# ScalarE and VectorE in written order for the first norm, squares on both engines, weight parts, and the small loads on GpSimd's queue

## The chip, the cores and the metric

The kernel runs on one core of one Trainium2 chip. The metric is the device time of one execution in microseconds (us), the median of several runs. A lower time is better.

## What is computed

One layer of a hybrid block over x of 512 x 1024 in float32. Cut to what matters:

```
xn = RMSNorm(x) * g_mix
u  = xn @ W_in                       # [q | k | v | rnn_x | rnn_gate | gate_A | gate_B], 1024 columns each
A  = chunked band attention(q, k, v) with a relative bias
xc = causal depthwise conv (width 4) of rnn_x, with bias
B  = RG-LRU(xc; block-diagonal gates W_r, W_i, softplus(-lambda)) * GeLU(rnn_gate)
mix = (sigmoid(gate_A) * (A @ W_a) + sigmoid(gate_B) * (B @ W_b)) @ W_o
h  = x + mix;  h = h + SwiGLU(RMSNorm(h));  out = RMSNorm(h)
```

## The kernel before

Every product is made of three matmuls on float32r parts: each operand is split into an upper part `hi` (rounded) and a lower part `lo = x - hi`, and `mm3` (L72 to L76) adds hi\*hi (L74), hi\*lo (L75) and lo\*hi (L76). `split` (L78 to L81) makes `hi` on ScalarE (L80) and `lo` on VectorE (L81). Weights come in chunks of 256 columns (`xr0`, `gr0`, `ga0`, `gb0`, `xr2` and so on), each in two loads of 4 x 128 rows; the tile of a split half chunk is `whl`, of which there are four buffers, that of its load is `raw`, of which there are three. So the halves of chunk `ga0` take the buffers that `xr0` had, and those of `gb0` the buffers of `gr0`, once TensorE has done with them.

The beginning goes like this. x comes in four tiles of 128 rows (`xt`). `squares` (L369) sums the squares of a tile on ScalarE; `norm_half` (L339) takes two tiles: square root on ScalarE (L334), reciprocal on VectorE (L336), scaling on VectorE (L345), transposes on TensorE (L353) into PSUM (`pt_mix`), then the upper part of `xnT` with the norm's weights on ScalarE (L357) and the lower part on VectorE (L358). As soon as the first 256 rows are there, `first_half` projects them with chunks `xr0` and `gr0` into four PSUM tiles (`po_xr` and `po_gr`, two columns of 128 each); the other 256 rows follow into the same tiles. Behind it the small vectors (`vr`: convolution, biases, lambda) are transposed (`vp`, L405) into `vc`, softplus of lambda is worked out in small steps (`sp_...`, L432 to L457), and the gates' block weights are split into `wrg_r` and `wrg_i` (upper part on ScalarE, L466, lower part on GpSimd, L467).

Then comes the loop over channels. `rnn_conv` (L477) makes the convolution `xc`: one tap on ScalarE (L483), three on VectorE (L485), each of which reads `po_xr` in PSUM. `rnn_gelu` (L491) works on `po_gr` (`g`). `rnn_gates` multiplies the parts of `xc` (`xch`, L487 and L488) with `wrg` into `rg`. The gate chunks `ga` and `gb` follow into PSUM tiles of the tag `mm`, which has four buffers: the first tile of `ga0` has the buffer of the first `po_xr`, so its first matmul waits until all taps of that `xc` are done.

What order an engine runs its instructions in is decided when the program is built: the framework's scheduler places them by its own estimates, keeping dependences, and each engine then goes through its row strictly in that order. TensorE's row is such a list too: an instruction that waits holds all behind it. SP issues the weight loads in order, and a load into a `raw` buffer waits there until the buffer is free.

Of the kernel before, what the change touches and what calls it, by code (L numbers as in the profile page):

```python
# [36 lines left out]
def block_kernel(ctx: ExitStack, tc: tile.TileContext, x, norm_mix_g, w_in, b_merge, rel_table,  # L37
# [28 lines left out]
    def f(ap):  # L66
        return ap.bitcast(F32)

    def mm_tile(name, tag="mm"):
        return ps.tile([P, S], F32, tag=tag, bufs=4 if tag == "mm" else 2, name=name)  # L70

    def mm3(o, sh, sl, mh, ml, start, stop, parts=False):  # L72

        pe.matmul(o, sh, mh, start=start, stop=False, skip_group_check=parts)  # L74
        pe.matmul(o, sh, ml, start=False, stop=False, skip_group_check=parts)  # L75
        pe.matmul(o, sl, mh, start=False, stop=stop, skip_group_check=parts)  # L76

    def split(hi, lo, src):  # L78

        act.activation(hi, src, AF.Copy)  # L80
        dve.tensor_sub(lo, src, f(hi))  # L81
# [242 lines left out]
    sp.dma_start(out=vr[V_CW:V_CW + 32, :], in_=conv_w.rearrange("w (t p) -> (w t) p", p=P))  # L324
    for at, vec, n in ((V_CB, conv_b, 8), (V_BR, b_rg_r, 8), (V_BI, b_rg_i, 8), (V_LAM, rg_lambda, 8), (V_BM, b_merge, 16),
                       (V_GF, norm_ffn_g, 8)):
        sp.dma_start(out=vr[at:at + n, :], in_=vec.rearrange("(t p) -> t p", p=P))
# [39 lines left out]
    ssq = []

    def squares(t):  # L369
        junk = nm.tile([P, D], F32, tag="junk", bufs=1, name=f"junk{t}")  # L370
        q = cp.tile([P, 1], F32, tag="ssq", bufs=4, name=f"ssq{t}")
        act.activation(junk[:], xt[t][:], AF.Square, accum_out=q[:])
        ssq.append(q[:])
# [7 lines left out]
    def xn_at(k, part, half):
        return xnT[k][:, part, half * 256:half * 256 + 256]

    squares(0)
    squares(1)
    norm_half(nm, xt, ssq, gm, xn_at, 0, "mix")
# [4 lines left out]
    def first_half(name):
        whl = weights(name, 0)
        for c in range(2):
            first[name, c] = mm_tile(f"po_{name}_{c}")
            project(first[name, c], whl, c, xnT, 0, 256)

    squares(2)
    squares(3)
    first_half("xr0")
    norm_half(nm, xt, ssq, gm, xn_at, 1, "mix")  # L400
    first_half("gr0")
# [61 lines left out]
    wrg = []  # L463
    for name, raw in zip("ri", wrg_raw):
        hl = rw2.tile([P, 2, 8, P], F32R, bufs=1, name=f"wrg_{name}")
        act.activation(hl[:, 0], raw[:], AF.Copy)  # L466
        pool.tensor_sub(hl[:, 1], raw[:], f(hl[:, 0]))  # L467
# [520 lines left out]
```

## Time and profile before

| | us |
|---|---|
| median of 3 runs | 886.83 (884.99 to 887.63) |
| the profiled execution, its own time | 887.36 |
| its span, from first to last instruction | 885.6 |
| TensorE busy (matmuls) | 873.6 |
| VectorE busy | 551.7 |
| ScalarE busy | 472.6 |
| GpSimd busy | 111.4 |

The span is what the profile sees; some 1.8 us lie around it. A row of the timeline names start, duration, engine (PE is TensorE, DVE is VectorE, ACT is ScalarE, POOL is GpSimd, SPq is the queue of SyncE), line, operation, the tile written and those read, the shape, a count, and in brackets the idle time ahead of it with what ended it. In a table by windows, the columns behind the engine's busy time are the granted clock (PEclk), the DMA share and GB/s. Matmuls overlap, so their distance from start to start says more than their duration.

### The profile page before, as it was taken

How to read it: one execution, taken by the hardware profiler on the slowest of the kernel's cores; microseconds unless marked ns; L12 is line 12 of the kernel's file. 1: busy time of each engine (PE TensorE's matmuls, PEld its weight loads, DVE VectorE, ACT ScalarE, POOL GpSimd, SP SyncE). 2: the span in 40 equal slices, each digit the busy share in tenths (PEclk: the TensorE clock that was granted, in tenths of full speed). 3: DMA queues.
4: the chain of work that ended last, by engine and by line, in shares of the span. 5: the costliest groups of instructions: out<-in, count | busy, mean ns of one | idle time of the engine just before them, and what ended most of it. 6: DMA issues, size and time to landing. Idle time of an engine off the chain costs nothing.

```text
span 885.6 us, 13331 instructions
## 1 busy us (share of the span) xinstructions
PE 873.6 (99%) x5220; PEld 778.1 (88%) x5220; DVE 551.7 (62%) x872; ACT 472.6 (53%) x839; POOL 111.4 (13%) x157
## 2 busy tenths in 40 slices
PE   8999999999999999999999999999999999999997
PEld 5988888888888989898888889999999999888886
DVE  5776557663456475765556556888878887553203
ACT  7566646652256485766633366656555555723203
POOL 4013111220022232222100000000000001300100
PEclk9999999999999999999999999999999999999999
DMA  8223233433333233232223720524333332353002
GB/s 266 86 82 104 86 95 94 122 95 95 97 96 93 61 96 96 72 108 72 62 84 121 258 75 22 165 74 126 113 95 96 100 128 84 119 180 126 27 1 95
DMA packets 86080, 90.10 MB, mean 102 GB/s; under 512 B 5377, under 2 KB 74609, under 8 KB 86017
## 3 DMA queue, kind: packets, MB, share of 16 engines
q1 hardware_dynamic: 84640, 85.78, 31.6%
q10 hardware_dynamic: 1376, 3.47, 1.0%
q8 instruction: 41, 0.67, 0.3%
q14 instruction: 23, 0.18, 0.1%
HBM read 87.10 MB, written 2.14 MB: 101 GB/s over the span
## 4 chain that ended last, share of the span: by engine, by line
PE 96%; DVE 2%; DMA 1%; ACT 1%; issue 0%; POOL 0%; ACTq 0%; DVEq 0%
PE po_out L75 5%; PE po_out L74 5%; PE po_out L76 5%; PE o L690 2%; PE p_fg L74 2%; PE p_fg L76 2%; PE p_fu L76 2%; PE p_fg L75 2%; PE p_fu L75 2%; PE p_fu L74 2%; PE pT L670 2%; PE po_v L74 2%; PE po_v L75 2%; PE po_v L76 2%; PE po_ga L74 2%; PE po_ga L75 2%
## 5 line engine op out<-in xcount | busy, mean ns | idle before, releaser
L75 PE MATMUL po_out<-whl_fo,act_hi 128*128 128x512 f32 (+1 forms) x198 | 72.5, 366 | 0.0
L74 PE MATMUL po_out<-whl_fo,act_hi 128*128 128x512 f32 (+1 forms) x198 | 72.3, 366 | 0.0
L76 PE MATMUL po_out<-whl_fo,act_lo 128*128 128x512 f32 (+1 forms) x198 | 71.7, 365 | 0.0
L81 DVE TENSOR_TENSOR whl_fo<-raw_fo,whl_fo 128x1024 fp32r<-128x1024 f32 x22 | 27.9, 1274 | 44.2 <-ACT whl_fo L80 43.8
L872 POOL TENSOR_TENSOR act_lo<-act,act_hi 128x1024 fp32r<-128x1024 f32 x4 | 10.9, 2718 | 325.2 <-ACT act_hi L871 323.2
L80 ACT ACTIVATE whl_fo<-raw_fo 128x1024 fp32r<-128x1024 f32 x22 | 23.0, 1057 | 49.0 <-PE po_out L76 35.4
L658 POOL TENSOR_SCALAR p<-p,rl 128x128 f32<-128x128 f32 (+1 forms) x64 | 35.1, 567 | 105.8 <-DVE rl L656 105.5
L655 ACT ACTIVATE p<-p,m 128x128 f32<-128x128 f32 (+2 forms) x64 | 35.7, 561 | 13.3 <-DVE m L654 12.9
L74 PEld LDWEIGHTS po_out<-whl_fo,act_hi 128*128 128x128 f32 x198 | 37.4, 189 | 6.1
L76 PEld LDWEIGHTS po_out<-whl_fo,act_lo 128*128 128x128 f32 x198 | 37.3, 189 | 6.0
L75 PEld LDWEIGHTS po_out<-whl_fo,act_hi 128*128 128x128 f32 x198 | 37.4, 189 | 5.9
L74 PE MATMUL po_v<-whl_v,xnT 128*128 128x256 f32 x128 | 36.7, 287 | 0.0
L75 PE MATMUL po_v<-whl_v,xnT 128*128 128x256 f32 x128 | 36.5, 285 | 0.0
L76 PE MATMUL po_v<-whl_v,xnT 128*128 128x256 f32 x128 | 36.5, 285 | 0.0
L654 DVE CUSTOM_DVE_ANT_0 p<-s,bias 128x128 f32<-128x128 f32 (+2 forms) x64 | 30.2, 487 | 8.8 <-PE s L652 8.1
L81 DVE TENSOR_TENSOR pp<-pT,pp 128x256 fp32r<-128x256 f32 (+2 forms) x64 | 29.1, 486 | 3.4 <-ACT pp L80 3.0
L75 PE MATMUL po_xr<-xnT,whl_xr 128*128 128x512 f32 (+1 forms) x80 | 27.9, 354 | 0.6 <-DVE xnT L358 0.6
L81 DVE TENSOR_TENSOR whl_fg_s<-s_fg,whl_fg_s 128x1024 fp32r<-128x1024 f32 x20 | 25.6, 1294 | 3.7 <-ACT whl_fg_s L80 3.7
L74 PE MATMUL po_gr<-xnT,whl_gr 128*128 128x512 f32 (+1 forms) x80 | 27.8, 349 | 0.1
L81 DVE TENSOR_TENSOR whl_qk<-raw_qk,whl_qk 128x1024 fp32r<-128x1024 f32 x16 | 20.0, 1250 | 12.5 <-ACT whl_qk L80 11.9
L76 PE MATMUL po_gr<-xnT,whl_gr 128*128 128x512 f32 (+1 forms) x80 | 27.5, 348 | 0.3 <-DVE whl_gr L81 0.3
L75 PE MATMUL po_gr<-xnT,whl_gr 128*128 128x512 f32 (+1 forms) x80 | 27.6, 346 | 0.0
(348 smaller groups left out, 3062.0 us busy)
## 6 DMA issues: line engine op xcount, KB each, us to landing
raw_fg<-in_w_ffn_in_dram SPq DMA_DIRECT2D x24, 512.0 KB, 4.5
raw_fu<-in_w_ffn_in_dram SPq DMA_DIRECT2D x22, 512.0 KB, 4.1
raw_fo<-in_w_ffn_out_dram SPq DMA_DIRECT2D x22, 512.0 KB, 4.3
raw_qk<-in_w_in_dram SPq DMA_DIRECT2D x32, 256.0 KB, 3.3
raw_xr<-in_w_in_dram SPq DMA_DIRECT2D x8, 512.0 KB, 4.5
raw_gr<-in_w_in_dram SPq DMA_DIRECT2D x8, 512.0 KB, 3.5
raw_ga<-in_w_in_dram SPq DMA_DIRECT2D x8, 512.0 KB, 3.6
raw_gb<-in_w_in_dram SPq DMA_DIRECT2D x8, 512.0 KB, 3.5
```

Of the source, the lines that this page charges most:

```text
L74: pe.matmul(o, sh, mh, start=start, stop=False, skip_group_check=parts)
L75: pe.matmul(o, sh, ml, start=False, stop=False, skip_group_check=parts)
L76: pe.matmul(o, sl, mh, start=False, stop=stop, skip_group_check=parts)
L80: act.activation(hi, src, AF.Copy)
L81: dve.tensor_sub(lo, src, f(hi))
L654: dve.tensor_tensor_reduce(prob[qb][:], sc[:, 0:w], bias[:, S - w:S], -1.0, 3e38, ALU.add, ALU.min, nmax[:, qb:qb + 1])
L655: act.activation(prob[qb][:], prob[qb][:], AF.Exp, bias=nmax[:, qb:qb + 1], scale=-1.0, accum_out=lsum[:, qb:qb + 1])
L658: pool.tensor_scalar(prob[qb][:], prob[qb][:], rl[:, qb:qb + 1], 1.0, ALU.mult, ALU.mult)
L670: pe.transpose(pt[:, at * P:(at + 1) * P], prob[qb][:, kb * P:(kb + 1) * P], ident[:])
L690: pe.matmul(po[:, S - n:S], st, pp[i][:, part, lo:lo + n], start=kb == 0 and part == 0, stop=kb == NT - 1 and part == 1)
L872: (pool if i in (0, 1, 2, 4) else dve).tensor_sub(lo[:], o[:], f(hi[:]))
```

## The change

It has five parts.

- The first norm and projections are written anew, with ScalarE and VectorE in program order (`manual_schedule`); the other engines are still placed by the scheduler. The squares of a pair of tiles are summed on both engines (`rstd_pair`), the square root and reciprocal are taken for the pair at once, and scaling is done in halves of 512 columns on both engines (`scaled`).
- Chunk `xr0` is split in four parts of two k-steps each, set between the transposed pairs (`chunk_in_parts`, `turned`); chunk `gr0` is split in two parts. `first_half` takes ranges of k-steps.
- The lower part of the second half of `xr0`, made by GpSimd, is made by VectorE.
- The seven small loads of `vr` are issued by GpSimd instead of SP.
- The upper parts of `wrg` are kept in program order on ScalarE. A fill tile of 48 floats a partition goes.

```diff
-                if len(made) == 0 and k:
-                    act.activation(hl[:, 0], raw[:], AF.Copy)
-                    pool.tensor_sub(hl[:, 1], raw[:], f(hl[:, 0]))
-                else:
-                    split(hl[:, 0], hl[:, 1], raw[:])
+                split(hl[:, 0], hl[:, 1], raw[:])
...
-        sp.dma_start(out=vr[at:at + n, :], in_=vec.rearrange("(t p) -> t p", p=P))
+        pool.dma_start(out=vr[at:at + n, :], in_=vec.rearrange("(t p) -> t p", p=P))
...
+    def rstd_pair(half):
+        q = cp.tile([P, 2], F32, name=f"ssq{half}")
+        junk = nm.tile([P, D], F32, tag="junk", bufs=1, name=f"junk{half}")
+        act.activation(junk[:], xt[2 * half][:], AF.Square, accum_out=q[:, 0:1])
+        junk = qkp.tile([P, D], F32, tag="qk", bufs=3, name=f"junkb{half}")
+        x_ = xt[2 * half + 1]
+        dve.tensor_tensor_reduce(junk[:], x_[:], x_[:], 1.0, 0.0, ALU.mult, ALU.add, q[:, 1:2])
+        sd = cp.tile([P, 2], F32, name=f"sdp{half}")
+        act.activation(sd[:], q[:], AF.Sqrt, bias=eps_t[:], scale=1.0 / D)
+        rs = cp.tile([P, 2], F32, name=f"rsp{half}")
+        dve.reciprocal(rs[:], sd[:])
+        return rs
...
+    with tc.manual_schedule(engines={mybir.EngineType.Activation, mybir.EngineType.DVE}):
+        rs = rstd_pair(0)
+        act.copy(gm[:], gm_p[:, 0:8])
+        xs = scaled(0, rs)
+        xr0 = chunk_in_parts("xr0")
+        xr0(0, 2)
+        turned(0, xs, 0)
+        xr0(2, 2)
+        turned(0, xs, 2)
+        first_half("xr0", range(0, 4))
+        xr0(4, 2)
+        turned(0, xs, 4)
+        xr0(6, 2)
+        turned(0, xs, 6)
+        first_half("xr0", range(4, 8))
+        gr0 = chunk_in_parts("gr0")
+        gr0(0, 4)
+        first_half("gr0", range(0, 4))
+        rs = rstd_pair(1)
+        xs = scaled(1, rs)
+        turned(1, xs, 0)
+        turned(1, xs, 2)
+        gr0(4, 4)
+        first_half("gr0", range(4, 8))
+        turned(1, xs, 4)
+        turned(1, xs, 6)
...
-        act.activation(hl[:, 0], raw[:], AF.Copy)
+        tc.keep_in_program_order(act.activation(hl[:, 0], raw[:], AF.Copy))
```

Behind the beginning (from the second pair of channels on) the rows of every engine are the same in both kernels, but for line numbers. Three places differ in what follows.

ScalarE, from the softplus on. In the rows' names the last number is a running one; `xc_481` and `xc_513` are the convolutions of channels 0 and 1, `whl_ga_0` and `whl_ga_4` the halves of chunk `ga0`. Before:

```order
L434 ACTIVATE sp_e<-sp_al 128x8
L483 ACTIVATE xc_481<-po_xr_0_225,vc 128x512
L80 ACTIVATE whl_ga_4_452<-raw_ga_4_453 128x1024
L483 ACTIVATE xc_513<-po_xr_1_250,vc 128x512
L494 ACTIVATE g_545<-po_gr_0_331 128x512
L80 ACTIVATE whl_gb_0_630<-raw_gb_0_631 128x1024
L487 ACTIVATE xch_486<-xc_481 128x512
L494 ACTIVATE g_594<-po_gr_1_356 128x512
L80 ACTIVATE whl_gb_4_635<-raw_gb_4_636 128x1024
```

The same stretch in the changed program:

```order
L489 ACTIVATE sp_e<-sp_al 128x8
L521 ACTIVATE wrg_r<-wrg_raw_r 128x1024
L521 ACTIVATE wrg_i<-wrg_raw_i 128x1024
L79 ACTIVATE whl_ga_4_452<-raw_ga_4_453 128x1024
L79 ACTIVATE whl_gb_0_630<-raw_gb_0_631 128x1024
L79 ACTIVATE whl_gb_4_635<-raw_gb_4_636 128x1024
L538 ACTIVATE xc_481<-po_xr_0_199,vc 128x512
L538 ACTIVATE xc_513<-po_xr_1_200,vc 128x512
L549 ACTIVATE g_545<-po_gr_0_275 128x512
```

The two `wrg` passes, which stood among the `xnT` passes of the first norm, and three weight passes now stand between `sp_e` and the first `xc`, where none stood.

VectorE, up to the third tap (128x509) of the first `xc`. Before:

```order
L442 TENSOR_TENSOR sp_s_403<-sp_s 128x8
L485 SCALAR_TENSOR_TENSOR xc_481<-po_xr_0_225,vc,xc_481 128x511
L444 TENSOR_SCALAR sp_p<-sp_s_403 128x8
L485 SCALAR_TENSOR_TENSOR xc_481<-po_xr_0_225,vc,xc_481 128x510
L446 TENSOR_TENSOR sp_p<-sp_p,sp_s_403 128x8
L81 TENSOR_TENSOR whl_ga_4_452<-raw_ga_4_453,whl_ga_4_452 128x1024
L485 SCALAR_TENSOR_TENSOR xc_481<-po_xr_0_225,vc,xc_481 128x509
```

Now, behind more of the small `sp` rows and the lower parts of `whl_ga_4` and `whl_gb_0`:

```order
L502 TENSOR_SCALAR sp_p<-sp_p 128x8
L80 TENSOR_TENSOR whl_gb_4_635<-raw_gb_4_636,whl_gb_4_635 128x1024
L501 TENSOR_TENSOR sp_p<-sp_p,sp_s_403 128x8
L540 SCALAR_TENSOR_TENSOR xc_481<-po_xr_0_199,vc,xc_481 128x511
L502 TENSOR_SCALAR sp_p<-sp_p 128x8
L540 SCALAR_TENSOR_TENSOR xc_513<-po_xr_1_200,vc,xc_513 128x511
L550 SCALAR_TENSOR_TENSOR g_545<-g_545,po_gr_0_275 128x512
L540 SCALAR_TENSOR_TENSOR xc_481<-po_xr_0_199,vc,xc_481 128x510
L503 TENSOR_TENSOR sp_p<-sp_p,sp_s_403 128x8
L550 SCALAR_TENSOR_TENSOR g_594<-g_594,po_gr_1_276 128x512
L540 SCALAR_TENSOR_TENSOR xc_513<-po_xr_1_200,vc,xc_513 128x510
L540 SCALAR_TENSOR_TENSOR xc_481<-po_xr_0_199,vc,xc_481 128x509
```

One subtraction of a weight stood ahead of that tap; now three do, and two taps of the other channel and two steps of `g`.

GpSimd, from the identity to `wrg`. Before:

```order
masks.py:199 AFFINE_SELECT ident<-ident 128x128
L237 TENSOR_TENSOR whl_xr_4_222<-raw_xr_4_130,whl_xr_4_222 128x1024
L416 COPY ext<-tab 16x384
L417 COPY ext<-tab 16x256
L467 TENSOR_TENSOR wrg_r<-wrg_raw_r,wrg_r 128x1024
L467 TENSOR_TENSOR wrg_i<-wrg_raw_i,wrg_i 128x1024
```

And now:

```order
L319 DMA vr<-in_conv_w_dram 32x128
masks.py:199 ISA
masks.py:199 AFFINE_SELECT ident<-ident 128x128
L322 DMA vr<-in_conv_b_dram 8x128
L322 DMA vr<-in_b_rg_r_dram 8x128
L322 DMA vr<-in_b_rg_i_dram 8x128
L322 DMA vr<-in_rg_lambda_dram 8x128
L322 DMA vr<-in_b_merge_dram 16x128
L322 DMA vr<-in_norm_ffn_g_dram 8x128
L471 COPY ext<-tab 16x384
L472 COPY ext<-tab 16x256
L522 TENSOR_TENSOR wrg_r<-wrg_raw_r,wrg_r 128x1024
```

The subtraction of `xr0` is gone from GpSimd's row, and seven loads stand in it, one of them ahead of the identity that every transpose needs. The `wrg` subtractions keep their place in this row, but each waits for ScalarE's pass.

More of the change, by code (lines that the diff above doesn't have):

```diff
@@ L365, in features @@
         return t, [t[:, k] for k in range(KT)]
[L367 to L373, printed above, removed]
     gm_p = ps.tile([P, S], F32, tag="s", bufs=2, name="gm_p")
@@ L377, in block_kernel @@
     gm = cp.tile([P, 8], F32, name="gm")
-    act.copy(gm[:], gm_p[:, 0:8])
     _, xnT = features(xnp, "xn", "xnT")
[L381 to L386, printed above, removed]
+    def rstd_pair(half):
[10 more added lines that the diff above has]
+        return rs
@@ new lines, in scaled @@
+    def scaled(half, rs):
+        xs = [nm.tile([P, D], F32, tag="xs", bufs=2, name=f"xs_mix{2 * half + i}") for i in range(2)]
+        for at, eng in ((slice(0, S), act), (slice(S, D), dve)):
+            dve.tensor_scalar(xs[0][:, at], xt[2 * half][:, at], rs[:, 0:1], None, ALU.mult)
+            if eng is act:
+                act.activation(xs[1][:, at], xt[2 * half + 1][:, at], AF.Copy, scale=rs[:, 1:2])
+            else:
+                dve.tensor_scalar(xs[1][:, at], xt[2 * half + 1][:, at], rs[:, 1:2], None, ALU.mult)
+        return xs
@@ new lines, in turned @@
+    def turned(half, xs, jp):
+        pt = ps.tile([P, 2, 256], F32, tag="t", bufs=2, name=f"pt_mix{half}_{jp}")
+        for i in range(2):
+            for j in range(2):
+                pe.transpose(pt[:, j, i * P:(i + 1) * P], xs[i][:, (jp + j) * P:(jp + j + 1) * P], ident[:])
+        for j in range(2):
+            g_ = gm[:, jp + j:jp + j + 1]
+            hi, lo = (xnT[jp + j][:, part, half * 256:half * 256 + 256] for part in range(2))
+            act.activation(hi, pt[:, j], AF.Identity, scale=g_)
+            dve.scalar_tensor_tensor(lo, pt[:, j], g_, f(hi), ALU.mult, ALU.subtract)
@@ new lines, in chunk_in_parts, with part @@
+    def chunk_in_parts(name):
+        tiles = [wp.tile([P, 2, 4, CW], F32R, tag="whl", bufs=4, name=f"whl_{name}_{k}") for k in (0, 4)]
+        def part(k, n):
+            if (name, k - k % 4) not in raws:
+                load(name, k - k % 4)
+            at = slice(k % 4, k % 4 + n)
+            split(tiles[k // 4][:, 0, at], tiles[k // 4][:, 1, at], raws[name, k - k % 4][:, at])
+            if at.stop == 4:
+                raws.pop((name, k - k % 4))
+        made.append(lambda part_, k, at: tiles[k // 4][:, part_, k % 4, at])
+        return part
@@ L389, in block_kernel, with first_half @@
     first = {}
-    def first_half(name):
-        whl = weights(name, 0)
+    def first_half(name, ks):
         for c in range(2):
[L394 to L401, printed above, removed]
+            if (name, c) not in first:
+                first[name, c] = mm_tile(f"po_{name}_{c}")
+        for k in ks:
+            for c in range(2):
+                at = slice(c * P, (c + 1) * P)
+                whl = made[index[name]]
+                mm3(first[name, c][:, 0:256], whl(0, k, at), whl(1, k, at),
+                    xnT[k][:, 0, 0:256], xnT[k][:, 1, 0:256], k == 0, k == KT - 1)
```

3 lines of the change are left out of this document (1 added, 2 removed).

## The prediction

> **What bounds the kernel now.** I read the page first: which engine is full, and which engine the chain of work that ended last runs through.
>
> ```profile
> PE 873.6 (99%) x5220; PEld 778.1 (88%) x5220; DVE 551.7 (62%) x872; ACT 472.6 (53%) x839; POOL 111.4 (13%) x157
> ...
> PE 96%; DVE 2%; DMA 1%; ACT 1%; issue 0%; POOL 0%; ACTq 0%; DVEq 0%
> ```
>
> TensorE is busy for 99% of the span and carries 96% of the chain. So the other engines count only where TensorE waits for them, and a hole made in TensorE's stream early is carried to the end, since nothing behind it is idle enough to take it up. The change touches the first 60 us only; behind that every engine's rows are the same in both kernels. I therefore looked at three points of TensorE's timeline: the first projection matmul, the transpose `vp`, and the first matmul of `po_ga`.
>
> ```profile
> 9.61 0.51 PE L74 MATMUL po_xr<-xnT,whl_xr 128*128 128x256 f32 x2 [0.41 <-ACT xnT L357]
> ...
> 32.28 0.24 PE L405 MATMUL vp<-ident,vr 88*128 88x88 f32 x1
> ...
> 38.15 0.28 PE L75 MATMUL po_gr<-xnT,whl_gr 128*128 128x256 f32 x1
> 38.27 0.28 PE L76 MATMUL po_gr<-xnT,whl_gr 128*128 128x256 f32 x1
> 38.87 0.47 PE L74 MATMUL po_ga<-xnT,whl_ga 128*128 128x512 f32 x1 [0.33 <-DVE sp_p L447]
> ```
>
> A 128x256 matmul is issued every 0.12 us. Between 9.61 and `vp` stand 142 of these and 24 transposes (in the changed order too); at 0.12 and about 0.11 us they fill 19.6 of 22.7 us, so some 3 us there are holes. Between `vp` and `po_ga` stand 50 matmuls, 6.0 us, without a hole. `po_ga` then waits for VectorE: it takes the PSUM buffer of `po_xr`, which the third tap of the convolution (L485, 128x509) has to have read. Here that tap ends at 38.72, and the wait is 0.6 us from matmul to matmul. **That wait is where I expect the time to go.**
>
> **The first norm and the first projections.** Squares on both engines: the second row of x decides.
>
> ```profile
> L295 SPq DMA_DIRECT2D x<-in_x_dram x2: 383/402/421, 0.7 to 1.2; - x2
> ...
> DMA to landing us min/median/max: 4.8/4.8/4.8
> ```
>
> ```profile
> 6.02 1.06 ACT L372 ACTIVATE junk<-x 128x1024 f32<-128x1024 f32 x1
> ```
>
> The second transfer starts at 1.2 and so lands at 6.0; ScalarE's second square starts at 6.02, so in before it waited for its data and not for ScalarE. A second engine for it gains nothing. The new square-and-sum on VectorE is a fused reduction like that of L654, which takes 0.69 us for 512 elements:
>
> ```profile
> L654 DVE CUSTOM_DVE_ANT_0 p<-s,bias 128x512 f32<-128x512 f32 x16 | 11.0, 688 | 4.5 <-PE s L652 4.3
> ```
>
> Twice that, 1.38, is the most for 1024; I take 1.3, and it ends at 7.3. One square root and one reciprocal for the pair (0.3 and 0.2) give 7.95; half of a row scaled on ScalarE 0.6, two transposes 0.45, one `xnT` pass 0.5, with the gaps between engines: the first matmul stands at about 9.75, 0.15 later than before. From there two k-steps take ScalarE, VectorE and ScalarE again in turn (a half weight pass, then two `xnT` passes, each of which waits for VectorE's part of the one ahead), about 2.1 us, for 1.9 us of matmuls and transposes. Four such pairs leave about 1.0 us of holes, the first lower parts 0.6, the whole `gr` chunk's lower part behind them 0.75, the second half's first `xnT` 0.7 and single steps the rest: 3.3 us, estimated so, against 3.0. `vp` moves to about **32.6, +0.3 us**; bounds 31.9 and 33.3. The split that leaves GpSimd, the `vr` loads that leave SP's queue (the weight load behind them can go out up to 3.2 us earlier, from 11.7 to 14.9; rows below) and the fill tile cost and gain nothing by themselves: ScalarE and VectorE, in their fixed order, are what is late there, and they cover these.
>
> **The stretch between `vp` and `po_ga`.** The last edit of the diff pins the `wrg` passes behind the softplus. With it, three things now stand ahead of the tap that were elsewhere. ScalarE first, with its rows from before:
>
> ```profile
> 34.36 0.21 ACT L434 ACTIVATE sp_e<-sp_al 128x8 f32<-128x8 f32 x1
> 34.48 0.76 ACT L483 ACTIVATE xc<-po_xr,vc 128x512 f32<-128x512 f32 x1
> 35.14 1.05 ACT L80 ACTIVATE whl_ga<-raw_ga 128x1024 fp32r<-128x1024 f32 x1
> 36.09 0.77 ACT L483 ACTIVATE xc<-po_xr,vc 128x512 f32<-128x512 f32 x1
> 36.75 0.59 ACT L494 ACTIVATE g<-po_gr 128x512 f32<-128x512 f32 x1
> 37.23 1.06 ACT L80 ACTIVATE whl_gb<-raw_gb 128x1024 fp32r<-128x1024 f32 x1
> ```
>
> From start to start a 1024-wide pass takes 0.95, `xc` 0.66, `g` 0.48. Call the start of `vp` V. `sp_e` is done, and ScalarE free, at V+2.2. Before, the first `xc` came next. Now `wrg_r`, `wrg_i`, `whl_ga` and the first `whl_gb` come, until V+6.0. The second `whl_gb` reuses the buffer of the last `gr` weights, so it waits for TensorE's last `gr` matmul: V+6.3 to 7.3. Only then `xc`: **V+7.3 instead of V+2.2**.
>
> VectorE and GpSimd next:
>
> ```profile
> 20.40 2.61 DVE L81 TENSOR_TENSOR whl_gr<-raw_gr,whl_gr 128x1024 fp32r<-128x1024 f32 x1
> ...
> 37.98 0.74 DVE L485 SCALAR_TENSOR_TENSOR xc<-po_xr,vc,xc 128x509 f32<-128x509 f32 x1
> ...
> 38.71 0.75 DVE L485 SCALAR_TENSOR_TENSOR xc<-po_xr,vc,xc 128x511 f32<-128x511 f32 x1
> 39.37 0.68 DVE L495 SCALAR_TENSOR_TENSOR g<-g,po_gr 128x512 f32<-128x512 f32 x1
> 39.97 1.94 DVE L81 TENSOR_TENSOR whl_gb<-raw_gb,whl_gb 128x1024 fp32r<-128x1024 f32 x1
> ...
> 43.16 1.21 DVE L81 TENSOR_TENSOR whl_gb<-raw_gb,whl_gb 128x1024 fp32r<-128x1024 f32 x1
> 44.30 0.16 DVE L447 TENSOR_SCALAR sp_p<-sp_p 128x8 f32<-128x8 f32 x1
> ```
>
> ```profile
> 16.74 2.41 POOL L467 TENSOR_TENSOR wrg_r<-wrg_raw_r,wrg_r 128x1024 fp32r<-128x1024 f32 x1 [2.17 <-ACT wrg_r L466]
> 19.10 2.83 POOL L467 TENSOR_TENSOR wrg_i<-wrg_raw_i,wrg_i 128x1024 fp32r<-128x1024 f32 x1
> 39.53 1.30 POOL L488 TENSOR_TENSOR xch<-xc,xch 128x512 fp32r<-128x512 f32 x1 [17.60 <-ACT xch L487]
> ```
>
> ```profile
> L446 DVE TENSOR_TENSOR sp_p<-sp_p,sp_s x6: 154/162/1204, 36.8 to 48.5; 128x8 f32<-128x8 f32 x6
> ```
>
> A subtraction `whl` takes VectorE 1.21. Where GpSimd's subtraction runs beside it, it ends 1.1 us after GpSimd has ended: 20.40+2.61 is 23.01, GpSimd's end 21.93; 39.97+1.94 is 41.91, GpSimd's end 40.83. So it stood still until GpSimd was done. An 8-wide `sp_p` product, 0.16, took 1.20 once. The Trainium skill, page "SBUF — State Buffer", section "Who interferes with whom", states that a VectorE instruction with two SBUF inputs contends with a GpSimd instruction that reads SBUF, and that the loser is blocked, not slowed; this trace agrees (1.08 us behind GpSimd's end, twice). By that rule the blocked 4.8 us below belong in the sum in full; if the two shared the port, about half of them would, and the sum would end some 2 us lower.
>
> In before GpSimd made the two `wrg` parts from 16.74 to 21.93, ahead of V. Now they follow ScalarE's `wrg` passes: V+3.3 to 5.7 and V+5.8 to 8.2, 2.41 each. VectorE has its `sp` row from V+2.3, about 0.2 each in turn; six are through by V+3.5, one gets in at V+5.7, and it is free at V+8.2. Then five small ones (V+9.1), `whl_ga` (1.14 start to start, from 43.16 and 44.30), two small, `whl_gb`, one small, `whl_gb`, one small: V+12.85. Then, in the new order, ahead of and with the third tap: five taps of 0.66, two `g` of 0.60, two small ones, 4.75 in all: V+17.6. `po_ga` starts at **V+17.7, 50.3 us, against 38.87: +11.4**. Without any blocking the row would stand at V+13.4 (the second `whl_gb` of ScalarE at V+7.35, then 1.14 and 4.9): 46.0, and with V at its low bound 45.3, +6.5. With V at 33.3 and 2.83 for one `wrg` it is +12.5. I take 11.4, since both rows with a clean end show blocking in full. Behind it: `xch` follows the tap within 0.6 us plus 1.3 on GpSimd, and `rg` stands 20 matmuls of 0.24, 4.8 us, behind `po_ga`; so no second wait.
>
> **The clock behind the hole.** TensorE stands still from V+6.3 to V+17.7. Before has one long hole of this kind, at 280.9:
>
> ```profile
> 280.47 0.40 PE L652 MATMUL s<-kl,q 128*128 128x512 f32 x1
> 282.22 1.56 PE L670 MATMUL pT<-ident,p 128*128 128x128 f32 x6 [1.36 <-POOL p L658]
> ```
>
> ```profile
> 280.30:283.60 3.30, 1.69 (x10) 1.00 0.51 158
> 283.70:287.00 3.30, 3.30 (x17) 0.50 0.24 46
> 287.20:290.00 2.80, 2.80 (x25) 1.00 0.15 36
> ```
>
> ```profile
> 1.19 6.57 PE L301 MATMUL busy<-idle 128*128 128x512 bf16 x16 [1.19 <-DVE eps_t L307]
> ```
>
> After 1.4 us without a matmul the granted clock was 0.50 for the next 3.3 us at least, and 17 instructions were done where 25 go into 2.8 us at full clock. From a cold start, the 16 matmuls of 512 columns took 6.57 us, 0.41 each, against 0.24 by the 0.12 for 256 columns above. So a hole of 11 us surely costs a stretch at half clock, of 3.4 to 6.6 us, half of which is lost: 1.7 to 3.3 us. I take **2.3**. The Trainium skill, page "TensorE: Matmul & The Clock Gate", Part 1, states that the clock halves after an idle window of about 3.4 us; here 1.4 us idle did it, so the measurement decides, and for 11 us both say the same.
>
> **Sum.** 0.3 + 11.1 + 2.3 = 13.7 on the profiled execution's own 887.36: 901.1. The median of the runs is 0.5 lower, so I give **900.5 us**.
>
> **Rivals.**
> 1. *The blocking is smaller than its two rows say* (VectorE gets in between GpSimd's passes): the hole is 6.5 to 8 us, plus 1.7 for the clock: 895 to 896.5. Against it are the two ends that agree to 0.01 us. Chance 0.10.
> 2. *Not slower: the third tap is in time.* Place: the PSUM buffer of `po_xr`. If the tap ends within 0.6 us of the last `gr` matmul, as in before, only the front counts, and with all its 3 us of holes closed the median would be 883.8; with none closed, 887. It decides at V+6.6, and for that ScalarE would have to run `xc` ahead of the weight passes. The built order has it behind them. Chance 0.06, half of it faster by over 0.3% (about what a measurement of this kernel can tell from no change), half within.
> 3. *The small loads on GpSimd's queue come late.* `vp` needs all seven. No row shows a load issued by GpSimd; the nearest are those that SP issued (the first and the last of seven), and GpSimd's row for the identity:
>
> ```profile
> 11.68 1.05 SPq L324 DMA_DIRECT2D vr<-in_conv_w_dram  x1
> 14.55 0.30 SPq L327 DMA_DIRECT2D vr<-in_norm_ffn_g_dram  x1
> ```
>
> ```profile
> 2.75 0.29 POOL masks.py:199 TENSOR_SCALAR_AFFINE_SELECT ident<-ident 128x128 f32<-128x128 f32 x1
> ```
>
>    On SP a load took 0.3 to 1.1 us of the queue. GpSimd is free from 2.75, so each may take 4.2 us before V moves; beyond that every us is one of the end, 904 and more. The identity, behind the first of them, is needed at 7.7. Chance 0.04.
>
> The forecast has 0.80, from 897 to 903.5 (V and the blocking at their bounds, 1.7 to 3.3 for the clock, 1 us for the runs' own spread). The range takes in most of the first rival: 895.5 to 903.5. Faster 0.03, within 0.3% 0.03, slower 0.94.
>
> **What would show it.** In the changed profile: `vp` between 31.9 and 33.3; the first `po_ga` near 50, with a wait of some 11 us put down to VectorE's `xc` or the row behind it; `wrg` on GpSimd right behind `sp_e`, and VectorE's 8-wide `sp_p` rows of over 2 us beside it; clock 0.50 for 3 to 7 us behind 45 to 50; from then on the same distances as before. A `po_ga` below 42 would make the whole reckoning wrong; a first matmul later than 10.5, or `vp` held by `vr`, the front's part of it.

## The result, and the profile after

The changed kernel takes 901.57 us (median of 4 runs, 900.82 to 901.98) against 886.93 beside it (4 runs, 884.99 to 887.63): the ratio is 1.0168, 95% interval 1.015 to 1.0185. So it is slower, by 14.6 us; 900.5 was forecast. (Of the runs of no_pin, below, one at 1235 us and a clock of 0.65 is left out.) The profiled execution of the changed kernel has an own time of 900.82 and a span of 899.0. Line numbers below are those of the changed kernel where the fence is of it or was made from it: its `mm3` is L73 to L75, `split` L79 and L80, the first tap of `xc` L538, the other taps L540, `wrg` L521 and L522, `vp` L460.

The page first, busy times and the shares of the chain that ended last.

```profile
PE 875.0 (97%) x5220; PEld 778.4 (87%) x5220; DVE 555.2 (62%) x879; ACT 472.3 (53%) x837; POOL 114.5 (13%) x163
...
PE 93%; DVE 2%; DMA 2%; ACT 1%; issue 1%; POOL 0%; SPq 0%; ACTq 0%; POOLq 0%; DVEq 0%
```

TensorE does the same 5220 instructions with 1.4 us more busy time, in a span that is 13.4 us longer: what came in is, but for these 1.4 us, idle time. Its waits between 30 and 62 us are one line, and its timeline has three rows to set against those of before (9.61, 32.28, 38.87).

```profile
PE po_ga L73 <- DVE xc L540: 11.7, 1, 11.7
```

```profile
9.90 0.50 PE L73 MATMUL po_xr<-xnT,whl_xr 128*128 128x256 f32 x2 [0.41 <-ACT xnT L401]
...
33.60 0.24 PE L460 MATMUL vp<-ident,vr 88*128 88x88 f32 x1
...
51.62 0.77 PE L73 MATMUL po_ga<-xnT,whl_ga 128*128 128x512 f32 x1 [11.75 <-DVE xc L540]
52.18 0.63 PE L74 MATMUL po_ga<-xnT,whl_ga 128*128 128x512 f32 x1
...
56.86 0.39 PE L73 MATMUL po_ga<-xnT,whl_ga 128*128 128x512 f32 x1
57.09 0.39 PE L74 MATMUL po_ga<-xnT,whl_ga 128*128 128x512 f32 x1
```

`vp` is 1.32 us later, `po_ga` 12.75. The 11.75 us in which TensorE stands still ahead of `po_ga` are called the hole below. Behind it 12 matmuls take 5.24 us (51.62 to 56.86), at a granted clock of 0.50 (the half clock), where they take 2.74 at full clock (12 x 0.228, the distance of the rows behind). The windows around the hole say the same (columns as in the prediction: start to end, width, then busy time and count of PE, PEld, DVE, ACT and POOL, then the granted clock).

```profile
39.00:43.00 4.00, 0.87 (x8) 0.67 (x6) 3.50 (x7) 3.78 (x6) 2.74 (x2) 1.00 0.01 2
43.20:51.60 8.40, 0.00 (x0) 0.01 (x1) 8.37 (x17) 1.37 (x4) 0.00 (x0) 0.50 0.63 187
51.70:56.80 5.10, 5.10 (x12) 4.07 (x13) 3.41 (x8) 1.12 (x2) 2.56 (x2) 0.50 0.00 1
57.00:60.00 3.00, 3.00 (x15) 2.47 (x14) 0.00 (x0) 0.00 (x0) 0.00 (x0) 1.00 0.00 0
```

While TensorE stands still, VectorE is busy for 8.37 of 8.40 us, and ScalarE hardly. Who holds VectorE back is in the rows between 35 and 51 us: ScalarE, GpSimd and VectorE.

```profile
35.69 0.21 ACT L489 ACTIVATE sp_e<-sp_al 128x8 f32<-128x8 f32 x1
35.80 1.04 ACT L521 ACTIVATE wrg_r<-wrg_raw_r 128x1024 fp32r<-128x1024 f32 x1
...
39.91 1.06 ACT L79 ACTIVATE whl_gb<-raw_gb 128x1024 fp32r<-128x1024 f32 x1 [0.22 <-PE po_gr L75]
40.87 1.43 ACT L538 ACTIVATE xc<-po_xr,vc 128x512 f32<-128x512 f32 x2
```

```profile
36.98 2.44 POOL L522 TENSOR_TENSOR wrg_r<-wrg_raw_r,wrg_r 128x1024 fp32r<-128x1024 f32 x1 [15.76 <-issue]
39.39 2.35 POOL L522 TENSOR_TENSOR wrg_i<-wrg_raw_i,wrg_i 128x1024 fp32r<-128x1024 f32 x1
```

```profile
36.97 0.17 DVE L501 TENSOR_TENSOR sp_p<-sp_p,sp_s 128x8 f32<-128x8 f32 x1
37.17 2.27 DVE L502 TENSOR_SCALAR sp_p<-sp_p 128x8 f32<-128x8 f32 x1
39.48 2.28 DVE L501 TENSOR_TENSOR sp_p<-sp_p,sp_s 128x8 f32<-128x8 f32 x1
...
42.91 1.23 DVE L80 TENSOR_TENSOR whl_ga<-raw_ga,whl_ga 128x1024 fp32r<-128x1024 f32 x1 [0.33 <-ACT g L549]
...
46.76 0.74 DVE L540 SCALAR_TENSOR_TENSOR xc<-po_xr,vc,xc 128x511 f32<-128x511 f32 x1
...
50.08 1.40 DVE L540 SCALAR_TENSOR_TENSOR xc<-po_xr,vc,xc 128x510 f32<-128x510 f32 x2
```

Two 8-wide steps, 0.17 each elsewhere, take 2.27 and 2.28 and end at 39.44 and 41.76, right behind GpSimd's two subtractions (39.42 and 41.74). Then come three lower parts of weights (42.91 to 46.77), and the taps and `g` behind them; the row of 1.40 holds two taps, and the second of them, the third of the first `xc`, ends at 51.48. At 51.62 `po_ga` starts. ScalarE's first `xc` had been ready since some 41.6 us; from 42.91 on VectorE has no wait, so what counts there is the work in its row ahead of that tap.

**Where the 13.46 us between the two profiled executions lie.** A fixed mark behind all this is the first matmul of `po_k`: 185.86 before, 201.04 after, 15.18 later. That is 12.75 for `po_ga`, and 2.43 remain, which fits the 2.50 that the half clock costs by the rows above. From there to the end 1.7 us come back: in before TensorE waits 1.36 us at 280.9 and then runs at clock 0.50 from 283.66 to 287.08, half of which 3.42 us is lost; in the changed kernel the same wait comes in two pieces and no half clock follows it. 12.75 + 2.43 - 1.7 = 13.5. The last term does not follow from the hole: pin_only, below, has nearly the same hole, and there the late wait is one piece of 1.37 us with a half clock behind it (295.50 to 298.92). What decides between one piece and two isn't shown.

```profile
185.86 0.39 PE L74 MATMUL po_k<-xnT,whl_qk 128*128 128x512 f32 x1
```

```profile
201.04 0.39 PE L73 MATMUL po_k<-xnT,whl_qk 128*128 128x512 f32 x1
```

```profile
PE pT L725 <- POOL p L713: 1.1, 2, 0.6
```

### The profile page after: what moved, and what is told of

Same layout as the page of the kernel before. It is cut to its first block, busy times and chain, and to the rows that moved or that the text cites. A ratio compares the mean times of both kernels' runs of the same rounds, so it can differ in the third digit from the quotient of the medians.

```text
span 899.0 us, 13348 instructions
## 1 busy us (share of the span) xinstructions
PE 875.0 (97%) x5220; PEld 778.4 (87%) x5220; DVE 555.2 (62%) x879; ACT 472.3 (53%) x837; POOL 114.5 (13%) x163
## 4 chain that ended last, share of the span: by engine, by line
PE 93%; DVE 2%; DMA 2%; ACT 1%; issue 1%; POOL 0%; SPq 0%; ACTq 0%; POOLq 0%; DVEq 0%
PE po_out L73 4%; PE po_out L74 4%; PE po_out L75 4%; PE p_fg L73 2%; PE o L745 2%; PE p_fg L75 2%; PE p_fg L74 2%; PE p_fu L75 2%; PE p_fu L74 2%; PE p_fu L73 2%; PE pT L725 2%; PE po_ga L73 2%; PE po_ga L74 2%; PE po_ga L75 2%; PE po_gr L75 2%; PE po_k L75 2%
## 5 line engine op out<-in xcount | busy, mean ns | idle before, releaser
L73 PE MATMUL po_out<-whl_fo,act_hi 128*128 128x512 f32 (+1 forms) x198 | 72.3, 366 | 0.0
L75 PE MATMUL po_out<-whl_fo,act_lo 128*128 128x512 f32 (+1 forms) x198 | 71.7, 365 | 0.0
L80 DVE TENSOR_TENSOR whl_fo<-raw_fo,whl_fo 128x1024 fp32r<-128x1024 f32 x22 | 27.8, 1274 | 44.2 <-ACT whl_fo L79 43.7
L79 ACT ACTIVATE whl_fo<-raw_fo 128x1024 fp32r<-128x1024 f32 x22 | 23.1, 1058 | 48.9 <-PE po_out L75 35.0
L75 PEld LDWEIGHTS po_out<-whl_fo,act_lo 128*128 128x128 f32 x198 | 37.3, 189 | 6.0
L73 PEld LDWEIGHTS po_out<-whl_fo,act_hi 128*128 128x128 f32 x198 | 37.4, 189 | 6.0
L73 PE MATMUL po_ga<-xnT,whl_ga 128*128 128x512 f32 x64 | 26.1, 408 | 11.7 <-DVE xc L540 11.7
L73 PE MATMUL po_v<-whl_v,xnT 128*128 128x256 f32 x128 | 36.3, 283 | 0.0
L75 PE MATMUL po_v<-whl_v,xnT 128*128 128x256 f32 x128 | 36.2, 283 | 0.0
L80 DVE TENSOR_TENSOR pp<-pT,pp 128x256 fp32r<-128x256 f32 (+2 forms) x64 | 29.1, 486 | 3.2 <-ACT pp L79 2.8
L75 PE MATMUL po_gr<-xnT,whl_gr 128*128 128x512 f32 (+1 forms) x80 | 27.5, 348 | 0.5 <-DVE whl_gr L80 0.5
L80 DVE TENSOR_TENSOR whl_fg_s<-s_fg,whl_fg_s 128x1024 fp32r<-128x1024 f32 x20 | 25.6, 1293 | 3.7 <-ACT whl_fg_s L79 3.7
L80 DVE TENSOR_TENSOR whl_qk<-raw_qk,whl_qk 128x1024 fp32r<-128x1024 f32 x16 | 20.0, 1250 | 12.5 <-ACT whl_qk L79 11.9
L73 PE MATMUL po_gr<-xnT,whl_gr 128*128 128x512 f32 (+1 forms) x80 | 27.6, 347 | 0.0
```

## The experiments

Theory: the pin (`keep_in_program_order` on ScalarE's two `wrg` passes) puts GpSimd's two subtractions and five weight passes of ScalarE (two of `wrg`, three of `whl`) between the softplus and the third tap; `po_ga` waits for that tap because it has the buffer of `po_xr`; the hole then costs a stretch at half clock besides. Rivals: the new front makes the hole; ScalarE alone does; VectorE is late as a whole and the wait would come back elsewhere; the half clock has another cause.

All times in us; "wait" is the idle time ahead of `po_ga`, "mark" the start of the first `po_k`, both from the profiled execution. The kernel before beside them had a median of 886.53 for the first four, 885.08 for the next four, 885.67 for the last four, so the ratio is the fairer column.

| kernel | vp | po_ga | wait | mark | median | ratio to before, 95% |
|---|---|---|---|---|---|---|
| before | 32.28 | 38.87 | 0.33 | 185.86 | 886.93 | |
| after | 33.60 | 51.62 | 11.75 | 201.04 | 901.57 | 1.0168 (1.015 to 1.0185) |
| no_pin | 36.29 | 44.14 | 1.58 | 191.14 | 891.92 | 1.0067 (1.0047 to 1.0088) |
| pin_only | 31.40 | 49.01 | 11.58 | 197.93 | 899.01 | 1.0148 (1.0133 to 1.0163) |
| fill_hole | 33.53 | 51.52 | 11.72 | 211.51 | 912.03 | 1.0291 (1.0273 to 1.031) |
| ga_other_buffer | 33.53 | 39.64 | 0 | 187.80 | 887.33 | 1.0017 (1.0006 to 1.0027) |
| fill_hole_2 | 33.44 | 51.45 | filled | 198.85 | 898.68 | 1.0153 (1.0135 to 1.017) |
| no_wrg_lower | 34.30 | 46.67 | 6.11 | 196.00 | 895.64 | 1.0118 (1.0099 to 1.0136) |
| wrg_lower_on_vector | 33.67 | 47.84 | 7.90 | 197.50 | 896.16 | 1.0124 (1.0098 to 1.0149) |
| free_order | 36.41 | 53.98 | 12.50 | 202.43 | 902.82 | 1.0197 (1.0179 to 1.0215) |
| old_front_mended | 31.33 | 37.19 | 0 | 184.10 | 885.22 | 0.999 (0.9979 to 1.0001) |
| new_front_mended | 33.60 | 39.71 | 0 | 186.62 | 887.42 | 1.0007 (0.9994 to 1.0019) |
| front_small_undone | 33.40 | 51.41 | 11.74 | 200.02 | 900.57 | 1.0167 (1.0149 to 1.0184) |
| xr_lower_on_gpsimd | 33.57 | 51.19 | 11.35 | 199.63 | 900.18 | 1.0163 (1.0144 to 1.0182) |

### The pin away, and the pin alone

The changed kernel without the pin:

```diff
-        tc.keep_in_program_order(act.activation(hl[:, 0], raw[:], AF.Copy))
+        act.activation(hl[:, 0], raw[:], AF.Copy)
```

> The changed kernel without the pin: the two wrg passes of ScalarE float ahead, into the first projections (as before the change). Theory (the pin makes the hole in front of po_ga, and without it the same 1.9 us of ScalarE and 4.8 us of a blocked VectorE fall into the fixed row of the first norm instead): vp at 35.5 to 36.5 instead of 33.60, po_ga 7.5 us behind it at 43 to 44 with a wait of 1 to 1.5 us instead of 11.75, no or a short stretch at half clock; time 890 to 893.5. Rival A (the pin is the whole loss, the new front costs nothing): vp 32 to 33, po_ga 39 to 40, time 886.5 to 888.5. Rival B (the hole comes from the new front and not from the pin): po_ga above 49, time 899 to 902.

Measured: the wait is 1.58, `vp` at 36.29, ratio 1.0067. The theory's numbers hold within 0.15 us: `vp` and the median (891.92) lie inside its ranges, `po_ga` (44.14) and the wait just above them. The 2.7 us by which `vp` moved are in the front, where ScalarE and VectorE keep the written order. There stand GpSimd's second subtraction, and VectorE's second square and sum (1.21 to 1.52 elsewhere):

```profile
19.19 3.38 POOL L522 TENSOR_TENSOR wrg_i<-wrg_raw_i,wrg_i 128x1024 fp32r<-128x1024 f32 x1
```

```profile
20.23 3.42 DVE L375 CUSTOM_DVE_ANT_0 junkb<-x 128x1024 f32<-128x1024 f32 x1
```

VectorE's piece ends at 23.65, 1.08 behind GpSimd's 22.57: blocked, and the second half of the norm waits for it. In the changed kernel this piece ends at 20.96, 2.69 earlier, which is all of the 2.7. So the pin isn't a pure loss: it keeps this out of the front.

The kernel before with nothing but the same pin:

> The kernel before with nothing but the pin. Theory (the pin alone makes the hole, whatever the front): vp falls to about 31 since the wrg passes are out of the front (32.28 before), po_ga 17.5 to 18 us behind it, at 48.5 to 49.5, wait of 11 to 12 us, then 12 matmuls at half clock; time 898 to 900. Rival B (the hole needs the new front): po_ga at 38 to 39, time 885.5 to 887.5.

Measured: `vp` 31.40, `po_ga` 49.01, ratio 1.0148.

```profile
31.40 0.24 PE L405 MATMUL vp<-ident,vr 88*128 88x88 f32 x1
49.01 0.77 PE L74 MATMUL po_ga<-xnT,whl_ga 128*128 128x512 f32 x1 [11.58 <-DVE sp_p L449]
```

From `vp` to `po_ga` it is 17.61, against 18.02 in the changed kernel and 6.59 before. The half clock behind it covers 9 to 10 matmuls, not the 12 expected. The pin alone makes the hole; the rival that needs the new front falls.

### The wait itself: another PSUM buffer

The changed kernel with `po_ga` in the two buffers of `vp` and the transposes:

```diff
-        po = tile_of(f"g{'ab'[w]}{j - j % 2}", j % 2)
+        po = tile_of(f"g{'ab'[w]}{j - j % 2}", j % 2, "t" if w == 0 and j < 2 else "mm")
```

> The changed kernel with the two tiles of po_ga in the PSUM buffers that vp and the transposes used, so that po_ga doesn't wait for the taps of the convolution to read po_xr; nothing else moves. Theory (the hole is the wait for that buffer, the weights are in time but for one lower part): po_ga 6.5 us behind vp, at 40 to 40.5, one wait of 0.5 to 1.5 us inside it for the lower part of the second whl_ga, no hole above 1.5 us later, no half clock; time 887 to 889.5. Rival (VectorE as a whole is late, and the wait comes back at po_gb or at rg, which need its whl_gb parts and the taps): a hole of 4 to 8 us at po_gb or rg, time 893 to 899.

Measured: `po_ga` at 39.64, straight behind the `gr` matmuls and 0.4 ahead of what was expected; one wait of 0.93, no later one up to 100 us; ratio 1.0017, mark 13.24 us earlier than in the changed kernel.

```profile
44.16 0.50 PE L75 MATMUL po_ga<-xnT,whl_ga 128*128 128x512 f32 x1 [0.93 <-DVE whl_ga L80]
```

```profile
37.11 2.27 DVE L502 TENSOR_SCALAR sp_p<-sp_p 128x8 f32<-128x8 f32 x1
39.42 2.33 DVE L501 TENSOR_TENSOR sp_p<-sp_p,sp_s 128x8 f32<-128x8 f32 x1
```

VectorE is blocked here just as long, and it costs under 1 us: `po_ga`'s own 48 matmuls, 11 us, cover it. The hole was the wait for a buffer; the blocked VectorE only set how long it lasted.

### What fills the time until the tap

The changed kernel with GpSimd writing zeros (the lower parts of `wrg` are left out), and with the two subtractions on VectorE:

```diff
-        pool.tensor_sub(hl[:, 1], raw[:], f(hl[:, 0]))
+        pool.memset(f(hl[:, 1]), 0.0)
```

```diff
-        pool.tensor_sub(hl[:, 1], raw[:], f(hl[:, 0]))
+        dve.tensor_sub(hl[:, 1], raw[:], f(hl[:, 0]))
```

> The changed kernel with GpSimd writing zeros in place of the two wrg subtractions: it leaves out the lower parts of wrg, and GpSimd then reads nothing beside VectorE. Theory (GpSimd's two subtractions block VectorE for the whole of their 4.8 us): the 8-wide sp_p rows of 2.27 us become 0.16, po_ga starts 12.5 to 13.5 us behind vp, at 46 to 47, wait of 6 to 7.5 us, half clock as before; time 896 to 897.5. Rival A (they are slowed and not blocked, or would fit elsewhere): po_ga 15 to 16 us behind vp, time 899 to 900. Rival B (ScalarE's late xc alone sets the end, the blocking lies beside it): po_ga at 51 to 51.6, time 901 to 902.

> The changed kernel with the two wrg subtractions on VectorE instead of GpSimd. Theory (VectorE loses 4.8 us to the blocking and would lose 2 times 1.14 to the work itself): po_ga 13.5 to 14.7 us behind vp, at 47 to 48.3, wait of 8 to 8.5 us; time 897.2 to 898.8. Rival (no full blocking): no gain or a loss of up to 2 us, 901 to 903.5.

Measured: `vp` to `po_ga` is 12.37 and 14.17 against 18.02, the waits 6.11 and 7.90: the theory's, with 12.37 and 7.90 just under its low ends (12.5 and 8). The medians, 895.64 and 896.16, are lower than it gave, but so was the kernel before beside them; their ratios on 886.93 give 897.4 and 897.9, inside. The gain is not blocking alone, though: the scheduler also set the rows anew. In no_wrg_lower VectorE makes both `whl_gb` parts among the taps and not ahead of them (first taps at 40.68, `whl_gb` at 43.98 and 46.44), and on ScalarE the first `xc` now stands ahead of one `whl_gb` (with the subtractions on VectorE) or both: counted from `vp` it starts 1.3 and 2.2 us earlier. Of the 5.65 us that no_wrg_lower gains, the two blocked rows account for 2 x 2.1; of the 3.85 us that the subtractions on VectorE gain, 4.2 less 2.3 of work. The remaining 1.5 and 2 us are put down to the order, which no run tests alone. ScalarE alone doesn't set the end: `po_ga` moved by more than its `xc` did. How long the hole would be with nothing but `xc` ahead of the weight passes isn't shown either.

### The clock

The changed kernel with extra matmuls that write a buffer nobody reads, behind the last `gr` matmul. The first try used the buffers of `rg`, and the scheduler put them behind the first matmuls of `rg`:

```diff
+            if j + c == 1:
+                fill = ps.tile([P, S], F32, tag="s", bufs=2, name="fill")
+                for _ in range(50):
+                    tc.keep_in_program_order(pe.matmul(fill[:], idle[:, 0:P], idle[:], start=True, stop=True))
```

> The changed kernel with 50 extra bf16 matmuls of 512 columns behind the last gr matmul, into a PSUM buffer that nothing reads: TensorE is busy in the hole, the hole for the real work stays. Theory (the half clock behind the hole comes from TensorE having stood still, and costs 2.4 to 2.6 us): po_ga at 51.6 as before within 0.3, granted clock 1.00 through and behind it, 0.23 from matmul to matmul at once; time 899 to 899.5 (901.57 less 2.5). Rival (the half clock has another cause, for instance the start of the full-size matmuls): 0.50 still stands behind po_ga, time 901 to 902.

It missed its question, since the hole was not filled:

```profile
51.52 0.77 PE L73 MATMUL po_ga<-xnT,whl_ga 128*128 128x512 f32 x1 [11.72 <-DVE xc L540]
...
64.69 10.97 PE L628 MATMUL fill<-idle 128*128 128x512 bf16 x49
```

It shows something else: 10.6 us more for TensorE (64.69 to the next row at 75.31) move the mark by 10.47 and the median by 10.46. What TensorE loses at this place is carried to the end. The second try, with tag "t" and 54 matmuls:

> The changed kernel with 54 extra bf16 matmuls of 512 columns, this time into the PSUM buffers of vp and the transposes, so that they stand between the last gr matmul and po_ga (0.22 us each by the run before, 11.6 us in all, the length of the hole). Theory (the half clock behind the hole comes from TensorE having stood still): po_ga at 51.6 within 0.4 (the first rg, which stands directly behind it in this order, may add 0.5), granted clock 1.00 behind it and 0.23 from matmul to matmul at once; time 898.8 to 900, 901.57 less 2.5 and up to 0.7 more for the row of rg. Rival (another cause): 0.50 behind po_ga, time 901.3 to 902.5.

```profile
39.60:51.40 11.80, 11.67 (x53) 5.15 (x54) 11.31 (x22) 4.63 (x8) 1.98 (x1) 1.00 0.44 134
51.40:57.00 5.60, 5.39 (x23) 4.28 (x24) 4.24 (x9) 3.79 (x6) 2.59 (x2) 1.00 0.00 0
```

`po_ga` stands at 51.45 as before, the clock is 1.00 throughout, and the mark is 2.19 us earlier (the row of `rg` directly behind took some tenths of it back). The median is 2.9 lower; its ratio, 1.0153, overlaps with that of the changed kernel, so the size rests on the trace. Standing still is the cause, the rival falls.

### The front

The changed kernel with the scheduler's order in the front, with two small edits undone, and with the lower parts of the second half of `xr` on GpSimd:

```diff
-    with tc.manual_schedule(engines={mybir.EngineType.Activation, mybir.EngineType.DVE}):
+    if True:
```

```diff
-        dve.tensor_tensor_reduce(junk[:], x_[:], x_[:], 1.0, 0.0, ALU.mult, ALU.add, q[:, 1:2])
+        act.activation(junk[:], x_[:], AF.Square, accum_out=q[:, 1:2])
...
-    pool.dma_start(out=vr[V_CW:V_CW + 32, :], in_=conv_w.rearrange("w (t p) -> (w t) p", p=P))
+    sp.dma_start(out=vr[V_CW:V_CW + 32, :], in_=conv_w.rearrange("w (t p) -> (w t) p", p=P))
```

```diff
+            o, raw = tiles[k // 4], raws[name, k - k % 4]
+            act.activation(o[:, 0, at], raw[:, at], AF.Copy)
+            (pool if name == "xr0" and k >= 4 else dve).tensor_sub(o[:, 1, at], raw[:, at], f(o[:, 0, at]))
```

> The changed kernel without the fixed order of ScalarE and VectorE in the first norm and projections (the scheduler orders them), all else kept, the pin too: it asks what moved vp to 33.60, which is 1.3 us behind before and 2.2 us behind the pin alone (31.40), where wrg is out of the front as well. Theory (the split in k-wise parts and the pair of squares cost it, the fixed order is right for them): vp 33.5 to 35, the rest as in the changed kernel, time 901.5 to 903. Rival (the fixed order costs it): vp at 31 to 32.5, time 898.8 to 900.5.

> The changed kernel with two of its small edits undone: the vr loads issued by SP again, and both squares of a pair on ScalarE. Theory (these two cost and gain nothing, the row of dependent steps between ScalarE and VectorE sets the front): vp within 0.4 of 33.60, or 0.5 to 0.8 later where the clock falls in the front; time within 1 of 901.57. Rival (the squares on VectorE, 1.23 and 1.52 us, or the loads on GpSimd hold the front): vp 0.8 to 1.5 us earlier, time 900 to 900.8.

> The changed kernel with the lower parts of the second half of the xr weights on GpSimd again, in two pieces of 512 elements. Theory of the prediction (the split that leaves GpSimd costs and gains nothing): vp within 0.4 of 33.60. Rival A (VectorE, with 0.69 more in each pair of k-steps, is what made vp later than reckoned): vp 0.4 to 1.0 us earlier, time 900.5 to 901.2. Rival B (two GpSimd pieces of 1.3 us block VectorE in the row): vp 0.5 to 1.5 later, time 902 to 903.

Measured: `vp` at 36.41, 33.40 and 33.57. In the scheduler's order `vp` is 2.8 us later, for code that is written in these parts; the theory gave 1.4 at most. The first matmul is at 10.70 there, and the clock is half from 12.8 to 19.6; how much of the 2.8 that half clock makes isn't shown (in new_front_mended, below, one from 10.7 to 14.1 left `vp` at 33.60). At the mark 1.4 is left of it: more `gr` work was done ahead of `vp`, so 1.2 us less stands behind it (5.07 us from there to `po_ga` besides the wait, 6.27 in the changed kernel), the wait is 0.75 longer, and the half clock behind the hole ends 2.1 us sooner, half of which is gained.

The squares and the small loads, undone in one run, move `vp` by 0.2: together they cost next to nothing, as forecast, and this run can't tell them apart. The split that left GpSimd moves it by 0.03, but that is two things of opposite sign. In xr_lower_on_gpsimd the load of `raw_xr` held ScalarE's first weight pass until 9.06 (8.49 in the changed kernel), and the four pairs of k-steps began 0.45 late (10.85 against 10.40). The last two pairs, whose lower parts were on GpSimd, then took 1.91 us each instead of 2.15, and at 16.82 the kernels were level. So by these rows the split on VectorE costs up to about 0.45 us at `vp` (an estimate), and not nothing; that is the low end of rival A, and the late load hid it.

That the marks of these two are 1.0 and 1.4 us earlier is mostly the clock: the half clock behind the hole ended 3.5 and 3.1 us after `po_ga` started, 5.2 in the changed kernel, which is worth 0.85 and 1.05; `po_ga` itself is 0.2 and 0.4 earlier. Their medians, 900.57 and 900.18, therefore decide nothing between theory and rivals.

### The version that the experiments point to

The kernel before with the pin, the subtractions on VectorE and `po_ga` in the other buffers; and the changed kernel with the last two.

> The kernel before with the pin, the two wrg subtractions on VectorE, and po_ga in the PSUM buffers of vp. Theory (the pin itself is a gain of 0.9 us, 31.40 against 32.28 at vp, and everything that it cost lay in the wait for po_xr's buffer and in the blocked VectorE): vp at 31.3 to 31.5, po_ga at 37.3 to 37.8 (38.87 before), no hole above 0.5 us up to 100 us, 1.0 to 1.6 us faster than the kernel before run beside it (ratio 0.998 to 0.999). Rival (the wait comes back later, at rg or po_gb, since VectorE has the same work in the same time): 1 to 5 us slower than before (ratio 1.001 to 1.006).

> The changed kernel with the same two mends (wrg subtractions on VectorE, po_ga in the PSUM buffers of vp); against the run of the kernel before so mended it shows the new first norm and projections alone. Theory (the new front makes vp 2.1 to 2.2 us later, 33.5 against 31.40, and nothing else): po_ga at 39.4 to 40.2, no later hole above 0.5 us, 1.8 to 2.4 us behind the mended kernel with the old front, 0.3 to 1.2 us slower than before (ratio 1.0003 to 1.0015). Rival (the new front's later vp is made up by work that it has already done): within 0.7 us of the mended kernel with the old front.

```profile
31.33 0.24 PE L405 MATMUL vp<-ident,vr 88*128 88x88 f32 x1
37.19 0.40 PE L74 MATMUL po_ga<-xnT,whl_ga 128*128 128x512 f32 x1
```

With the old front `po_ga` stands at 37.19 without a wait, the mark 1.76 us ahead of before. The ratio is 0.999 (0.9979 to 1.0001): a gain that 12 runs don't set apart from none; by the medians it is 0.45 us, where 1.0 to 1.6 was expected. Sorted by granted clock it is clearer: at 0.999 or more the mended kernel has 883.04 to 883.70 (4 runs), before beside it 884.59 to 885.63 (5 runs). That is a reading made afterwards, and the interval stands. With the new front the mark is 2.52 later and the median 2.2, ratio 1.0007: the new front by itself costs some 2.2 us, nothing of it made up later. The two intervals just overlap, so this size rests on the trace.

## Why the prediction was right, point by point

**What bounds.** Right: TensorE's idle time is the loss, and it stays to the end (fill_hole: 10.6 in, 10.46 out).

**The first norm.** The second row of x again set the start: VectorE's square starts at 6.00, on the landing, and takes 1.23 (1.3 taken). The first matmul is at 9.90 (9.75). That the squares and the small loads together cost nothing was right, by front_small_undone; that the split costs nothing was not, by the rows of xr_lower_on_gpsimd (up to about 0.45). The working's 7.95 for the end of the reciprocal is 0.15 more than its terms (7.3 + 0.3 + 0.2), a gap that it doesn't name; the row ends at 7.83.

```profile
6.00 1.23 DVE L375 CUSTOM_DVE_ANT_0 junkb<-x 128x1024 f32<-128x1024 f32 x1 [4.86 <-DMA x<-in_x_dram]
...
19.44 1.52 DVE L375 CUSTOM_DVE_ANT_0 junkb<-x 128x1024 f32<-128x1024 f32 x1
```

**`vp`.** The step that failed in size: "+0.3", bounds 31.9 and 33.3, measured 33.60, +1.3. The pairs of k-steps ran as reckoned (2.15 each, 2.1 taken), and the first matmul was 0.15 later than reckoned. The rest is holes. Counted with the prediction's own 0.12 for a matmul and 0.11 for a transpose, they come to some 4.0 us instead of 3.3 (an estimate from the rows): 1.8 to 1.9 while the first half takes `xr` (1.6 reckoned, with the first lower parts), 0.8 to 0.9 ahead of `gr`'s lower part (0.75), 0.5 at the second half's first `xnT` (0.7), 0.7 behind it (0.25). So no one wait was left out; small ones in the first pairs and behind the second half's norm were taken too small. The second square (1.52 on VectorE behind a weight part) isn't the reason, since `vp` comes only 0.2 earlier without it. The prediction also set two things of opposite sign into one number: the pin takes the `wrg` passes out of the front, -0.9 (pin_only, 31.40), and the new front costs 2.2 (33.60 against 31.40).

**Between `vp` and `po_ga`.** Right nearly row by row, counted from `vp`: `xc` at +7.27 (7.3 forecast), GpSimd at +3.38 to 5.82 and +5.79 to 8.14 (3.3 to 5.7, 5.8 to 8.2), VectorE free at +8.2 (8.2), `po_ga` at +18.02 (17.7). That blocking goes in in full was right: two rows of 2.27 and 2.28, which end within 0.02 us of GpSimd's two. The Trainium skill, page "SBUF — State Buffer", section "Who interferes with whom", has the loser blocked and not slowed, and has a scalar-operand instruction of VectorE contend too when it uses both port pairs; this trace agrees on the first. The first blocked row is a TENSOR_SCALAR with one input, which fits the second; which ports it used no run here shows. But the weight I gave the blocking was too simple: in ga_other_buffer the same blocked rows cost less than 1 us.

**The clock.** 2.3 taken, 2.43 at the mark, 2.5 by the rows, 2.19 by fill_hole_2. What wasn't in the sum: the half clock at 283.66 of before doesn't come in the changed kernel, 1.7 back. Since pin_only has nearly the same hole and does have that half clock, the hole is not what keeps it away; the cause stays open.

**Sum.** Against the forecast of 900.5: `vp` +1.0, the stretch behind it +0.3, clock +0.1, the late half clock -1.7, and the median lies 0.75 above the profiled execution where 0.5 below was taken, +1.25: together +1.0, and 901.57 was measured (the forecast itself was rounded down by 0.06). The mechanism was right; that the total is nearer than its terms was luck, since two misses of over 1 us cancelled a third.

**The rivals.** Smaller blocking: no, two rows. Tap in time: no, `xc` stood behind the weight passes as built. Loads on GpSimd late: no. The first and the last of seven, on GpSimd, are issued by 6.79, and `vp` comes only 0.2 earlier with them on SP (and both squares on ScalarE).

```profile
2.66 0.74 POOL L319 DMA_DIRECT2D vr<-in_conv_w_dram  x1
...
6.28 0.51 POOL L322 DMA_DIRECT2D vr<-in_norm_ffn_g_dram  x1
```

## What to carry to other kernels

Before weighing a moved piece of work, ask which buffer the next instruction of the full engine takes, and what must have read it: here 11 us hung on one PSUM buffer, and giving the tile another one took back nearly all, with every other delay still in place. A pin that keeps work out of one busy stretch puts it into another; price both ends apart, against the kernel with the pin alone, and not as one difference. GpSimd beside VectorE is no free help: the same 2.3 us of subtractions (2 x 1.14) on VectorE itself were cheaper than the 4.2 us for which its two blocked rows stood still.
